# A chunk-of-four layout for the state-space scan, whole rest splits and earlier tables in a two-layer trunk

## The chip, the cores and the metric

The kernel runs on one core of a Trainium2 chip. The time is the device time of one execution in microseconds, the median of three runs. The core has five engines that run side by side: TensorE (PE, matmuls; its weight loads are listed apart as PEld), VectorE (DVE), ScalarE (ACT), GpSimd (POOL), and SyncE (SP), which here does nothing but issue transfers between DRAM and on-chip memory. Each engine works through its own queue in program order and waits on semaphores for the others.

## The reference

Two layers work on `x` of 256 positions by 2048 features. Each has one input projection whose columns feed two groups of heads, a GLU projection, an output projection and two RMSNorms. Cut to what matters here:

```
for l in range(DEPTH):                                   # 2 layers
    h = rmsnorm(x, pre_norm_g[l])
    q, k, v, z_att, u, z_ssm = split(h @ w_in[l])        # 2048 x 6144
    o_att = diff_attention(q, k, v, lam, rel_bias)       # 8 heads, two softmax maps each
    o_att = rmsnorm(o_att, subln_g[l]) * (1 - lam_init) * silu(z_att)
    y = s5_ssm(u, ...)                                   # 64 groups x 64 complex states
    g_val, g_gate = split(gelu(y) @ w_glu[l])
    o_ssm = g_val * sigmoid(g_gate) * silu(z_ssm)
    mix = concat(o_att, o_ssm) @ w_out[l]
    x = x + rmsnorm(mix, post_norm_g[l])

s5_ssm:  h[t] = a * h[t-1] + B u[t]   (a, h complex, t = 0..255),   y = Re(C h) + d * u
```

## The kernel before

**Precision and the half steps.** Weights and activations are float32, and the kernel multiplies them in three products of rounded parts: high part by high part, high by rest, rest by high. Weights stream once from DRAM in 512 KB pieces called half steps, 144 a layer (`s` = 0 to 143), 288 in all (`hs`). Per half step SP loads `raw`, six half steps ahead (`emit_dma(hs + 6)`, five buffers); ACT rounds it into `hi` (`emit_hi(hs + 2)`); DVE forms the rest `lo = raw - hi` (`emit_lo(hs + 2)`, lines 245 to 264); PE runs `main(hs)`: 24 matmuls of 256 columns for s below 48, 12 of 512 columns after. The order of a layer is u (s 0 to 15), q (16 to 31), k (32 to 47), v and za, zs, the GLU weights, the output weights. The activations are `hthi`/`htlo` in the first projection, `ghi`/`glo` for GLU, `mxhi`/`mxlo` for the output.

**What sets the order.** The instruction order of each engine is written out by the Python program. Side work (tables, attention, scan, normalisation) sits in generators: `hooks(l, s)` (lines 1081 to 1133) starts them at given half steps, `run_first` and `run_second` (lines 302 to 318) let each go on by a piece before and behind `main`. Work of DVE in many small operations (the scan, the tables `z_ops` and `g_ops`) is put in a list `weave`; `fill` (line 213) takes operations from it until a budget in estimated nanoseconds is spent. In the loop over `hs` (lines 1229 to 1232) the budget `bal` is what PE is expected to take less what DVE has been given already. When there is anything to weave, `lo` is formed in two operations of 512 columns with side work ahead, between and behind.

**The state-space part.** 256 positions are cut in 64 chunks of 4. The evacuation of `u` (line 919 on) writes the projected `u` by chunk; `u_store` (line 680) sends half of it to a DRAM tile `uds` (s = 11 and 17), and `u_load` (line 684) brings it back in eight transfers as `U`, laid out by channel group (s = 12 and 18). `prep_gen` builds tables from the layer's parameters: `wi` (from u to each chunk's contribution to the state) and `gc` (from state to y, `g_ops`, line 611, whose operations in layer 0 wait for `cmfree`). `s_gen` (line 718, started at s = 15) multiplies `U` by `wi` on PE into `pss`, in four groups of 64 matmuls, and ACT copies each into `H`: for every state 64 chunks. The last two groups wait for `u2` (s >= 20). `scan_ops` (line 753) then runs over the 64 chunks one after another, in 62 steps of four operations of 128 x 64, each reading chunk s-1 at a stride of 64 words. `y_gen` (line 766) turns `H` and `gc` into y, and ends in `ghi` and `glo`, one operation of 512 columns each. `pt` and `apow` hold powers of `a`, made once at the start for both layers in `pow_ops` (line 459).

Of the kernel before, what the change touches and what calls it, by code (L numbers as in the profile page):

```python
# [10 lines left out]
F32 = mybir.dt.float32  # L11
# [14 lines left out]
MAGIC = 12582912.0  # L26
SC = 70
Y0 = (80, 77)
# [3 lines left out]
PG = 1  # L32
CAP = 1500.0
RES = 0.0
SA = 51
# [4 lines left out]
PD = (1, 1)  # L40
F0 = 7
EB = 400
W3 = 4
# [15 lines left out]
def hybrid_trunk(ctx: ExitStack, tc, x, rel_bias, pre_norm_g, post_norm_g, w_in, lambda_q1, lambda_k1,  # L59
# [40 lines left out]
    def cost(o):  # L100
        n = 1
        for d in o.shape[1:]:
            n *= d
        load[0] += 68 + n / 0.96
        return 68 + n / 0.96

# [8 lines left out]
    def tt(o, a, b, op):  # L115
        V.tensor_tensor(o, a, b, op=op)  # L116
        return cost(o)
# [23 lines left out]
    apow = cp.tile([128, 2, 64, 4], F32, name="apow")  # L141
    a4s = cp.tile([128, 2, 64], F32, name="a4s")
    cf = cp.tile([128, 2, 64], F32, name="cf")
    nlam = cp.tile([128, 2], F32, name="nlam")
# [100 lines left out]
    def emit_lo(hs, budget, halves=False):  # L245
        if hs >= 2 * NCH:
            return
        src, hi = raw.pop(hs), split[hs][0]
        lo = late[hs] if hs in late else sp.tile([128, 1024], F32R, tag="lo", name="lo")
        hf = hi.bitcast(F32)  # L250
        if (weave and budget > 0) or urgent:
            budget = UB if urgent else budget
            fill(budget / 3)
            for p in range(2):
                c = slice(512 * p, 512 * p + 512)
                tt(lo[:, c], src[:, c], hf[:, c], ALU.subtract)
                fill(budget / 3)
        elif halves:
            for p in range(2):
                c = slice(512 * p, 512 * p + 512)  # L260
                tt(lo[:, c], src[:, c], hf[:, c], ALU.subtract)
        else:
            tt(lo, src, hf, ALU.subtract)
        split[hs] = (hi, lo)
# [133 lines left out]
    def params_ops(T, bt):  # L398
# [72 lines left out]
        S["pw"] = True  # L471

        lm = bt[0:2, 1536:1664].rearrange("p (a d) -> p a d", a=2)
        lv = bt[0:2, 512:768].rearrange("p (a b d) -> p a b d", a=2, b=2)
# [10 lines left out]
    def prep_gen(l, slots):  # L485
# [45 lines left out]
        weave.append(z_ops(l, bv, zt, tcn))  # L531
        if l:
            weave.append(g_ops(l, ccv, tcn, gslots))
        yield from until("z" + K)
# [16 lines left out]
        if l:  # L551
            yield from until("g" + K)
        else:
            weave.append(g_ops(l, ccv, tcn, gslots))
        wi = []
# [3 lines left out]
        for b0 in range(0, 8, nb):  # L559
# [11 lines left out]
            for b, ps in zip(range(b0, b0 + nb), pss):  # L571
                psv = ps.rearrange("p (h a g q) -> p h a g q", h=2, a=2, g=2)
                wv = wi[b // 4].rearrange("p (b h r a q) -> p b h r a q", b=4, h=2, r=2, a=2)[:, b % 4]
                for r in range(2):
                    for g in range(2):
                        act(wv[64 * g:64 * g + 64, :, r], psv[64 * r:64 * r + 64, :, :, g ^ r], AF.Copy)
            if l and b0 == WB - 1:
                for _ in range(WY):
                    yield
# [31 lines left out]
    def g_ops(l, ccv, tcn, gslots):  # L611
        while f"cmfree{l}" not in S:
            yield 100
        apl = [apow[:, a, 32 * l:32 * l + 32, :] for a in range(2)]
        gs = []
        for hf in range(2):
            gc = R(gslots[hf], "gc")
            gv = gc.rearrange("p (m a e c) -> p m a e c", m=16, a=2, e=4)
# [99 lines left out]
    def s_gen(l):  # L718
        yield from until(f"wi{l}")
        H = rp.tile([128, 2, NPAIR, 64], F32, tag="big", name="H")  # L720
# [3 lines left out]
        for b0 in range(0, 8, 2):  # L724
            while b0 >= 4 and not S["u2"]:
                yield
# [3 lines left out]
            for b in (b0, b0 + 1):  # L730
                wi = S[f"wi{l}"][b // 4]
                for h in range(2):
# [6 lines left out]
            for r, ps in enumerate(pss):  # L739
                psv = ps.rearrange("p (a j c) -> p a j c", a=2, j=4)  # L740
                act(H[:, :, 4 * b0 + r:4 * b0 + 8:2, 1:64], psv[:, :, :, 0:63], AF.Copy)
        yield
# [3 lines left out]
        for d in range(2):  # L746
# [3 lines left out]
            yield  # L750
        weave.append(scan_ops(l))

    def scan_ops(l):
        H = S["H"]
        ar = apow[:, 0, 32 * l:32 * l + 32, 3].unsqueeze(1).to_broadcast([128, 2, 32])
        ai = a4s[:, :, 32 * l:32 * l + 32]
        for s in range(2, 64):
            t1 = scp.tile([128, 2, 32], F32, tag="sc1", name="sc1")
            t2 = scp.tile([128, 2, 32], F32, tag="sc2", name="sc2")
            yield mul(t1, H[:, :, :, s - 1], ar) + SC  # L760
            yield mul(t2, H[:, ::-1, :, s - 1], ai)
            yield tt(t1, t1, H[:, :, :, s], ALU.add) + SC
            yield tt(H[:, :, :, s], t1, t2, ALU.add) + SC
        S[f"h{l}"] = True

    def y_gen(l, j):
# [43 lines left out]
        yield  # L810
        hv = S["ghi"].rearrange("p (b c i) -> p i b c", b=8, i=4)[:, :, 2 * j:2 * j + 2]
        lv = S["glo"].rearrange("p (b c i) -> p i b c", b=8, i=4)[:, :, 2 * j:2 * j + 2]
        yv = pg.rearrange("p (i b c) -> p i b c", i=4, b=2)
        act(hv, yv, AF.Copy)
        tt(lv, yv, hv.bitcast(F32), ALU.subtract)
        S[f"y{l}{j}"] = True
# [102 lines left out]
    def evac(l, seg, b, ac):  # L919
        if seg in ("U4", "u"):  # L920
            yield from until(f"rbc{l}")
            for j, a in enumerate(ac):
                bb = j if seg == "U4" else b
                o = S["u"].rearrange("p (m b c) -> p b c m", m=4, b=8)[:, bb]
                mul(o, a[:, 0:256].rearrange("p (c m) -> p c m", m=4),
                    rbc.rearrange("p (c m) -> p c m", m=4))
        elif seg in ("q", "k"):
# [153 lines left out]
    def hooks(l, s):  # L1081
# [20 lines left out]
        if s == 96 and l + 1 < DEPTH:  # L1102
            S["prep"] = prep_gen(l + 1, (8, (8, 2), (4, 3)))
            at(cur[0], S["prep"])
# [5 lines left out]
        if s == 11:  # L1110
            S["U"] = rp.tile([128, NPAIR, 64], F32, tag="U", name="U")
        if s in (11, 17):
            u_store(0 if s == 11 else 4)
        if s in (12, 18):
            u_load(0 if s == 12 else 4)
        if s == 15:
            at(cur[0], s_gen(l))
        if s == 21:
            at(cur[0], toep_gen(l))
        S["u2"] = s >= 20  # L1120
        S["zfree"] = s >= 113
# [18 lines left out]
    cur = [0]  # L1140
    BUDS = (2250.0, 2200.0)
    BUDL = 2140.0
    with tc.manual_schedule():
# [26 lines left out]
        at(PG, params_gen())  # L1170
        at(2, prep_gen(0, (3, (1, 7), (4, 8))))
        S["done"] = None
        bal = 0.0
        for hs in range(2 * NCH):
# [53 lines left out]
            run_first(hs)  # L1228
            bal = min(bal, CAP) + (BUDL if not l and s >= 44 else BUDS[l]) + pload[0] - load[0] - 1130
            load[0] = 0.0  # L1230
            emit_lo(hs + 2, 0 if s >= SX else min(bal, EB) if s < F0 else bal - RES)
            bal -= max(0.0, load[0] - 1130)
            held = hs in late or 2 * LAYER - LB <= hs < 2 * LAYER
# [57 lines left out]
```

## Time and profile before

| what | us |
|---|---|
| median of three runs | 926.35 (925.54 to 928.47) |
| profiled execution, of that its span | 926.7, 924.9 |
| PE busy, share of the span | 907.7, 98% |
| DVE busy, share of the span | 683.5, 74% |
| ACT busy, share of the span | 488.1, 53% |
| mean granted clock of TensorE | 0.994 |

The rows further down come from one profiled execution; its span runs from the first to the last instruction. "Busy" of an engine adds the time of its instructions and leaves out those that only issue transfers or signal. A row's idle time is what the engine spent waiting just ahead of it, with the engine and tile that ended the wait. The granted clock is given as a share of 2.4 GHz, so 0.5 is 1.2 GHz.

### The profile page before, as it was taken

What the parts mean: (1) busy time and instruction counts of PE and PEld (TensorE: products, weight loads), DVE (VectorE), ACT (ScalarE), POOL (GpSimd) and SP (SyncE); (2) the same over time, 40 slices, a digit from 0 to 9 for tenths busy, and PEclk for the clock granted to TensorE, in tenths of its full rate; (3) what the DMA queues carried; (4) which work ended last, traced back from release to release, by engine and by line L of the source; (5) the groups of instructions that cost most, each with busy time, mean ns of one, the idle gap of its engine ahead of it and who ended that gap; (6) DMA issues with size and microseconds to landing.
All of it is one profiled execution on the core that took longest, in us unless ns stands there. A gap on an engine that the chain in (4) does not pass through costs nothing.

```text
span 924.9 us, 17644 instructions
## 1 busy us (share of the span) xinstructions
PE 907.7 (98%) x6722; PEld 795.1 (86%) x6722; DVE 683.5 (74%) x1606; ACT 488.1 (53%) x881; POOL 17.2 (2%) x26
## 2 busy tenths in 40 slices
PE   9999999999999999999999999999999999999995
PEld 8999999888888788887889999997888788888884
DVE  4898686999995756877877449999966566665564
ACT  6643384455465667444468443335565655644451
POOL 3000000000000000000000000000000000000001
PEclk9999999999999999999999999999999999999998
DMA  9988656855654497576656866965556346665852
GB/s 303 209 231 244 185 165 172 278 158 168 184 155 137 126 232 243 171 249 201 215 173 193 230 175 168 246 187 165 163 156 183 115 137 203 197 210 168 291 183 91
DMA packets 187892, 177.21 MB, mean 192 GB/s; under 512 B 42550, under 2 KB 131184, under 8 KB 186912
## 3 DMA queue, kind: packets, MB, share of 16 engines
q1 hardware_dynamic: 187456, 175.96, 64.3%
q8 instruction: 53, 0.87, 0.4%
q14 instruction: 31, 0.25, 0.1%
q0 software_dynamic: 352, 0.13, 0.1%
HBM read 168.44 MB, written 7.88 MB: 191 GB/s over the span
## 4 chain that ended last, share of the span: by engine, by line
PE 87%; DVE 5%; ACT 3%; DMA 2%; SPq 1%; issue 1%; DVEq 0%; ACTq 0%
PE ac L113 79%; DVE lo L116 2%; DMA xt<-in_x_dram 1%; PE lga L113 1%; PE psy L113 1%; PE pss L113 1%; PE po L113 1%; SPq L496 1%; PE psw L97 1%; PE acu L113 1%; ACT junk L134 1%; DMA raw<-in_w_glu_dram 1%; ACT hi L134 1%; DMA raw<-in_w_in_dram 1%; ACT y L134 0%
## 5 line engine op out<-in xcount | busy, mean ns | idle before, releaser
L134 ACT ACTIVATE hi<-raw 128x1024 fp32r<-128x1024 f32 (+1 forms) x282 | 297.8, 1056 | 357.3 <-PE ac L113 272.2
L116 DVE TENSOR_TENSOR lo<-raw,hi 128x512 fp32r<-128x512 f32 (+1 forms) x401 | 359.8, 901 | 105.5 <-ACT hi L134 104.3
L113 PE MATMUL ac<-hthi,hi 128*128 128x256 f32 x736 | 211.7, 288 | 0.3 <-ACT hi L134 0.3
L113 PE MATMUL ac<-htlo,hi 128*128 128x256 f32 x736 | 209.4, 285 | 0.8 <-DVE htlo L123 0.5
L113 PE MATMUL ac<-hthi,lo 128*128 128x256 f32 x736 | 209.1, 284 | 0.6 <-DVE lo L116 0.5
L113 PE MATMUL ac<-hi,hthi 128*128 128x512 f32 x384 | 154.4, 402 | 0.0
L113 PE MATMUL ac<-lo,hthi 128*128 128x512 f32 x384 | 149.8, 390 | 0.4 <-DVE lo L116 0.4
L113 PE MATMUL ac<-hi,htlo 128*128 128x512 f32 x384 | 150.1, 391 | 0.0
L113 PEld LDWEIGHTS ac<-htlo,hi 128*128 128x128 f32 x736 | 141.8, 193 | 1.7 <-DVE htlo L123 1.7
L113 PEld LDWEIGHTS ac<-hthi,hi 128*128 128x128 f32 x736 | 141.7, 193 | 1.3 <-ACT hi L134 0.5
L113 PEld LDWEIGHTS ac<-hthi,lo 128*128 128x128 f32 x736 | 141.7, 193 | 1.2 <-DVE lo L116 1.2
L113 PE MATMUL ac<-lo,mxhi 128*128 128x512 f32 x228 | 89.0, 390 | 0.7 <-DVE lo L116 0.6
L113 PE MATMUL ac<-hi,mxhi 128*128 128x512 f32 x228 | 89.0, 391 | 0.0
L113 PE MATMUL ac<-hi,mxlo 128*128 128x512 f32 x228 | 88.7, 389 | 0.0
L113 PEld LDWEIGHTS ac<-hi,hthi 128*128 128x128 f32 x384 | 72.1, 188 | 16.1
L113 PEld LDWEIGHTS ac<-hi,htlo 128*128 128x128 f32 x384 | 72.1, 188 | 15.8
L113 PEld LDWEIGHTS ac<-lo,hthi 128*128 128x128 f32 x384 | 72.2, 188 | 14.6 <-DVE lo L116 0.8
L113 PEld LDWEIGHTS ac<-lo,mxhi 128*128 128x128 f32 x228 | 42.8, 188 | 10.3 <-DVE lo L116 1.5
L113 PE MATMUL ac<-hi,ghi 128*128 128x512 f32 x128 | 51.5, 403 | 0.0
L113 PEld LDWEIGHTS ac<-hi,mxlo 128*128 128x128 f32 x228 | 42.8, 188 | 8.9
L113 PE MATMUL ac<-lo,ghi 128*128 128x512 f32 x128 | 50.1, 391 | 0.3 <-DVE lo L116 0.3
L113 PEld LDWEIGHTS ac<-hi,mxhi 128*128 128x128 f32 x228 | 42.8, 188 | 8.9
(206 smaller groups left out, 1154.5 us busy)
## 6 DMA issues: line engine op xcount, KB each, us to landing
raw<-in_w_in_dram SPq DMA_DIRECT2D x191, 512.0 KB, 4.2
raw<-in_w_out_dram SPq DMA_DIRECT2D x64, 512.0 KB, 4.7
raw<-in_w_glu_dram SPq DMA_DIRECT2D x32, 512.0 KB, 4.3
U<-uds SPq DMA_DIRECT2D x48, 64.0 KB, 3.3
xt<-in_x_dram SPq DMA_DIRECT2D x8, 256.0 KB, 7.6
uds<-u SPq DMA_DIRECT2D x4, 512.0 KB, 6.0
pg<-in_post_norm_g_dram SPq DMA_DIRECT2D x2, 1024.0 KB, 7.1
xt<-in_x_dram SPq DMA_DIRECT2D x2, 1024.0 KB, 10.1
```

The source lines that it names most:

```text
L97: P.transpose(o, i, idn)
L113: P.matmul(o, lhsT=l, rhs=r, start=start, stop=stop, skip_group_check=True)
L116: V.tensor_tensor(o, a, b, op=op)
L134: A.activation(out=o, in_=i, func=f, **kw)
L496: SY.dma_start(out=bv[64 * d:64 * d + 64, a, r::2], in_=src[l].rearrange("(m r g) p c -> r g p m c", r=2, g=2)[r, d ^ r])
```

## The change

Five things change. The 64 chunks are laid out in `H` by their place in groups of four (position `i` in the four, then group `k`): the evacuation of `u` writes that order, and the copies to `H`, the writing of `ghi` and `glo` follow it. `scan_ops` then first joins the four chunks of each group for all 16 groups at once (12 operations of 128 x 1024 and a small copy), steps over the 16 groups (15 steps of four operations of 128 x 64, with `a16`, the 16th power, made by nine more operations in `pow_ops`), and finally carries the group states back into the chunks (12 operations of some 1024). `lo` is formed by one operation also while there is work to weave. The budget of DVE counts 147 ns and 1/0.955 ns a column for each operation, its cap is 1800, and separate settings for the first half steps go. `g_ops` follows `z_ops` directly, and only its second half waits for `cmfree`; `s_gen` waits for the first half of `wi` only (`wa`). The hooks move: `u_store` to s = 14 and 19, `u_load` to s = 15 and 20, `u2` to s >= 22.

On SP in layer 1, from the last loads of `raw` ahead of the first store of `u` to those behind the second load of `U`, the kernel before has:

```order
L206 DMA raw<-in_w_in_dram 128x8x128 x8
L682 DMA uds<-u 512x1x256
L206 DMA raw<-in_w_in_dram 128x8x128
L691 DMA U<-uds 16x4x256 x8
L206 DMA raw<-in_w_in_dram 128x8x128 x5
L682 DMA uds<-u 512x1x256
L206 DMA raw<-in_w_in_dram 128x8x128
L691 DMA U<-uds 16x4x256 x8
L206 DMA raw<-in_w_in_dram 128x8x128 x5
```

In the changed kernel the same place reads:

```order
L204 DMA raw<-in_w_in_dram 128x8x128 x11
L686 DMA uds<-u 512x1x256
L204 DMA raw<-in_w_in_dram 128x8x128
L695 DMA U<-uds 16x4x256 x8
L204 DMA raw<-in_w_in_dram 128x8x128 x4
L686 DMA uds<-u 512x1x256
L204 DMA raw<-in_w_in_dram 128x8x128
L695 DMA U<-uds 16x4x256 x8
L204 DMA raw<-in_w_in_dram 128x8x128 x3
```

Three more loads of `raw` stand ahead of the first store, and four in place of five between the first load of `U` and the second store.

On PE in the changed kernel, at the end of half step 159 (s = 15 of layer 1), where `pss` first reads `U` in that layer:

```order
L110 MATMUL ac<-hthi,hi 128x256
L110 MATMUL ac<-htlo,hi 128x256
L110 MATMUL ac<-hthi,lo 128x256
L110 MATMUL pss<-U,wi 64x64 x32
L110 MATMUL ac<-hthi,hi 128x256
L110 MATMUL ac<-htlo,hi 128x256
```

The group of `pss` has the same place as in the kernel before, behind the same half step; the second pair of groups stands two half steps later than before.

On DVE at the start of layer 0's scan (`sc` are its two temporaries, `k` the evacuation of a projection), the kernel before has:

```order
L116 TENSOR_TENSOR lo<-raw,hi 128x1024
L116 TENSOR_TENSOR sc_2293<-H,apow 128x64
L116 TENSOR_TENSOR sc_2294<-H,a4s 128x64
L116 TENSOR_TENSOR sc_2293<-sc_2293,H 128x64
L116 TENSOR_TENSOR H<-sc_2293,sc_2294 128x64
L116 TENSOR_TENSOR sc_2299<-H,apow 128x64
L116 TENSOR_TENSOR lo<-raw,hi 128x512
```

and the changed kernel (`sct` holds the joined groups):

```order
L113 TENSOR_TENSOR sct<-H,a4s 128x1024
L113 TENSOR_TENSOR sct<-H,apow 128x1024
L113 TENSOR_TENSOR lo<-raw,hi 128x1024
L113 TENSOR_TENSOR sct<-sct,H 128x1024
L113 TENSOR_TENSOR sct<-sct 128x1024
L120 SCALAR_TENSOR_TENSOR k<-ac,rbc 128x256
L113 TENSOR_TENSOR lo<-raw,hi 128x1024
```

About two wide operations of the scan now stand between one `lo` and the next, and `lo` is whole.

```diff
...
@@ -101,8 +98,8 @@
         n = 1
         for d in o.shape[1:]:
             n *= d
-        load[0] += 68 + n / 0.96
-        return 68 + n / 0.96
+        load[0] += 147 + n / 0.955
+        return 147 + n / 0.955
 
     def mm4(o, l, r, start, stop):
         n, m = r.shape[-1], l.shape[-1]
...
@@ -250,11 +248,9 @@
         hf = hi.bitcast(F32)
         if (weave and budget > 0) or urgent:
             budget = UB if urgent else budget
-            fill(budget / 3)
-            for p in range(2):
-                c = slice(512 * p, 512 * p + 512)
-                tt(lo[:, c], src[:, c], hf[:, c], ALU.subtract)
-                fill(budget / 3)
+            fill(budget / 2)
+            tt(lo, src, hf, ALU.subtract)
+            fill(budget / 2)
         elif halves:
             for p in range(2):
                 c = slice(512 * p, 512 * p + 512)
@@ -469,6 +465,15 @@
         V.tensor_copy(a4s[:, 1], pi[3])
         yield ts(a4s[:, 0], pi[3], -1.0, None, ALU.mult)
         S["pw"] = True
+
+        sr, si = pr[3], pi[3]
+        for dr, di in ((T("tt"), T("tn")), (a16[:, 0], a16[:, 2])):
+            yield mul(T("p2"), sr, sr)
+            yield mul(T("p3"), si, si)
+            yield tt(dr, T("p2"), T("p3"), ALU.subtract)
+            yield stt(di, sr, 2.0, si, ALU.mult, ALU.mult)
+            sr, si = dr, di
+        yield ts(a16[:, 1], a16[:, 2], -1.0, None, ALU.mult)
 
         lm = bt[0:2, 1536:1664].rearrange("p (a d) -> p a d", a=2)
         lv = bt[0:2, 512:768].rearrange("p (a b d) -> p a b d", a=2, b=2)
@@ -529,8 +534,7 @@
             zt = [R(5, "z0"), R(6, "z1")]
         tcn = R(cslot, "ztmp")
         weave.append(z_ops(l, bv, zt, tcn))
-        if l:
-            weave.append(g_ops(l, ccv, tcn, gslots))
+        weave.append(g_ops(l, ccv, tcn, gslots))
         yield from until("z" + K)
         yield 1
         ps = side("pst")
@@ -550,8 +554,6 @@
         S["cmfree" + K] = True
         if l:
             yield from until("g" + K)
-        else:
-            weave.append(g_ops(l, ccv, tcn, gslots))
         wi = []
         while l and not S["wfree"]:
             yield
...
@@ -609,11 +613,11 @@
         S[f"z{l}"] = True
 
     def g_ops(l, ccv, tcn, gslots):
-        while f"cmfree{l}" not in S:
-            yield 100
         apl = [apow[:, a, 32 * l:32 * l + 32, :] for a in range(2)]
         gs = []
         for hf in range(2):
+            while hf and f"cmfree{l}" not in S:
+                yield 100
             gc = R(gslots[hf], "gc")
             gv = gc.rearrange("p (m a e c) -> p m a e c", m=16, a=2, e=4)
             ms = slice(16 * hf, 16 * hf + 16)
@@ -716,19 +720,19 @@
         yield
 
     def s_gen(l):
-        yield from until(f"wi{l}")
+        yield from until(f"wa{l}")
         H = rp.tile([128, 2, NPAIR, 64], F32, tag="big", name="H")
         S["H"] = H
         G.memset(H[:, :, :, 0:1], 0.0)
         U = S["U"]
         for b0 in range(0, 8, 2):
-            while b0 >= 4 and not S["u2"]:
+            while b0 >= 4 and not (S["u2"] and f"wi{l}" in S):
                 yield
             yield 2
 
             pss = [side("pss") for _ in range(2)]
             for b in (b0, b0 + 1):
-                wi = S[f"wi{l}"][b // 4]
+                wi = S[f"wi{l}" if b >= 4 else f"wa{l}"][b // 4]
                 for h in range(2):
                     for a in range(2):
                         for r, g in ((0, 0), (1, 1), (1, 0), (0, 1)):
@@ -738,7 +742,10 @@
             yield
             for r, ps in enumerate(pss):
                 psv = ps.rearrange("p (a j c) -> p a j c", a=2, j=4)
-                act(H[:, :, 4 * b0 + r:4 * b0 + 8:2, 1:64], psv[:, :, :, 0:63], AF.Copy)
+                hv = H[:, :, 4 * b0 + r:4 * b0 + 8:2]
+                act(hv[:, :, :, 16:64], psv[:, :, :, 0:48], AF.Copy)
+                act(hv[:, :, :, 1:16], psv[:, :, :, 48:63], AF.Copy)
+        weave.append(scan_ops(l))
         yield
 
         src = uds.rearrange("(q g n) (m r) -> g m n q r", q=4, g=2, m=4)
@@ -748,19 +755,41 @@
                 r = 64 * d + 16 * m
                 SY.dma_start(out=dst[r:r + 16, 1::2], in_=src[1 - d, m, :, 1::2])
             yield
-        weave.append(scan_ops(l))
 
     def scan_ops(l):
+
+
         H = S["H"]
-        ar = apow[:, 0, 32 * l:32 * l + 32, 3].unsqueeze(1).to_broadcast([128, 2, 32])
-        ai = a4s[:, :, 32 * l:32 * l + 32]
-        for s in range(2, 64):
+        c = slice(32 * l, 32 * l + 32)
+        ar = apow[:, 0, c, 3].unsqueeze(1).unsqueeze(3).to_broadcast([128, 2, 32, 16])
+        ai = a4s[:, :, c].unsqueeze(3).to_broadcast([128, 2, 32, 16])
+        br = a16[:, 0, c].unsqueeze(1).to_broadcast([128, 2, 32])
+        bi = a16[:, 1:3, c]
+        sct = R((3, 8)[l], "sct")
+        T, u = (sct[:, 1024 * i:1024 * i + 1024].rearrange("p (a m k) -> p a m k", a=2, m=32) for i in range(2))
+        h = [H[:, :, :, 16 * i:16 * i + 16] for i in range(4)]
+        prev = h[0]
+        for i in range(1, 4):
+            yield mul(u, prev[:, ::-1], ai)
+            yield mul(T, prev, ar)
+            yield tt(u, u, h[i], ALU.add)
+            yield tt(T, T, u, ALU.add)
+            prev = T
+        V.tensor_copy(h[3][:, :, :, 0], T[:, :, :, 0])
+        yield 140
+        for k in range(1, 16):
             t1 = scp.tile([128, 2, 32], F32, tag="sc1", name="sc1")
             t2 = scp.tile([128, 2, 32], F32, tag="sc2", name="sc2")
-            yield mul(t1, H[:, :, :, s - 1], ar) + SC
-            yield mul(t2, H[:, ::-1, :, s - 1], ai)
-            yield tt(t1, t1, H[:, :, :, s], ALU.add) + SC
-            yield tt(H[:, :, :, s], t1, t2, ALU.add) + SC
+            yield mul(t1, h[3][:, :, :, k - 1], br) + SC
+            yield mul(t2, h[3][:, ::-1, :, k - 1], bi)
+            yield tt(t1, t1, T[:, :, :, k], ALU.add) + SC
+            yield tt(h[3][:, :, :, k], t1, t2, ALU.add) + SC
+        for i in range(3):
+            p, o, n = (h[i - 1], h[i], 16) if i else (h[3][:, :, :, 0:15], h[0][:, :, :, 1:16], 15)
+            yield mul(u[:, :, :, 0:n], p[:, ::-1], ai[:, :, :, 0:n])
+            yield mul(T[:, :, :, 0:n], p, ar[:, :, :, 0:n])
+            yield tt(o, o, u[:, :, :, 0:n], ALU.add)
+            yield tt(o, o, T[:, :, :, 0:n], ALU.add)
         S[f"h{l}"] = True
 
     def y_gen(l, j):
...
@@ -921,9 +951,9 @@
             yield from until(f"rbc{l}")
             for j, a in enumerate(ac):
                 bb = j if seg == "U4" else b
-                o = S["u"].rearrange("p (m b c) -> p b c m", m=4, b=8)[:, bb]
-                mul(o, a[:, 0:256].rearrange("p (c m) -> p c m", m=4),
-                    rbc.rearrange("p (c m) -> p c m", m=4))
+                o = S["u"].rearrange("p (m b e k) -> p b k e m", m=4, b=8, e=4)[:, bb]
+                cut = lambda t: t.rearrange("p (k e m) -> p k e m", e=4, m=4)
+                mul(o, cut(a[:, 0:256]), cut(rbc))
         elif seg in ("q", "k"):
             stt(S[seg][:, 256 * b:256 * b + 256], ac[0][:, 0:256], 0.125 if seg == "q" else 1.0, rbc, ALU.mult, ALU.mult)
         elif seg == "v":
...
@@ -1109,15 +1139,15 @@
                 SY.dma_start(out=S["xt"][t], in_=src[128 * t:128 * t + 128])
         if s == 11:
             S["U"] = rp.tile([128, NPAIR, 64], F32, tag="U", name="U")
-        if s in (11, 17):
-            u_store(0 if s == 11 else 4)
-        if s in (12, 18):
-            u_load(0 if s == 12 else 4)
+        if s in (14, 19):
+            u_store(0 if s == 14 else 4)
+        if s in (15, 20):
+            u_load(0 if s == 15 else 4)
         if s == 15:
             at(cur[0], s_gen(l))
         if s == 21:
             at(cur[0], toep_gen(l))
-        S["u2"] = s >= 20
+        S["u2"] = s >= 22
         S["zfree"] = s >= 113
         S["wfree"] = l > 0
         for h in range(8):
...
@@ -1226,10 +1256,10 @@
                 if s < 3:
                     residual(l - 1, 512 * s + 512, 256)
             run_first(hs)
-            bal = min(bal, CAP) + (BUDL if not l and s >= 44 else BUDS[l]) + pload[0] - load[0] - 1130
+            bal = min(bal, CAP) + (2880.0 if s < 48 else 2724.0) - SPARE[2 if l else int(s >= 44)] + pload[0] - load[0] - LOT
             load[0] = 0.0
-            emit_lo(hs + 2, 0 if s >= SX else min(bal, EB) if s < F0 else bal - RES)
-            bal -= max(0.0, load[0] - 1130)
+            emit_lo(hs + 2, 0 if s >= SX else bal)
+            bal -= max(0.0, load[0] - LOT)
             held = hs in late or 2 * LAYER - LB <= hs < 2 * LAYER
             main(hs, 0 if held else None)
             pload[0] = 0.0
```

## Rows read from the trace of the kernel before

**Rows 1.** The page: span, busy time of each engine, shares of the chain, one issue group.

```profile
span 924.9 us, 17644 instructions
PE 907.7 (98%) x6722; PEld 795.1 (86%) x6722; DVE 683.5 (74%) x1606; ACT 488.1 (53%) x881; POOL 17.2 (2%) x26
...
PE 87%; DVE 5%; ACT 3%; DMA 2%; SPq 1%; issue 1%; DVEq 0%; ACTq 0%
...
uds<-u SPq DMA_DIRECT2D x4, 512.0 KB, 6.0
```

**Rows 2.** Waits of PE's weight loads: what for, us in total, times, longest.

```profile
PEld ac L113 <- DVE lo L116: 4.2, 7, 1.0
...
PEld po L113 <- ACT wt L134: 2.0, 2, 1.4
PEld psx L97 <- DVE xt L123: 1.7, 1, 1.7
...
PEld ac L113 <- DVE htlo L123: 1.7, 4, 0.7
```

**Rows 3.** Windows: stretch, length, busy PE, PEld, DVE, ACT, POOL; clock, DMA share, GB/s.

```profile
157.00:270.00 113.00, 113.00 (x577) 93.44 (x576) 109.73 (x411) 59.68 (x121) 0.52 (x1) 1.00 0.63 192
...
560.00:660.00 100.00, 100.00 (x696) 92.15 (x695) 96.85 (x338) 44.38 (x68) 0.00 (x0) 1.00 0.68 189
```

**Rows 4.** Timeline of SP's queue, 507 to 541 us: start, duration, issue, count.

```profile
508.84 0.37 SPq L206 DMA_DIRECT2D raw<-in_w_in_dram  x1
509.27 0.58 SPq L682 DMA_DIRECT2D uds<-u  x1
...
514.52 4.05 SPq L691 DMA_DIRECT2D U<-uds  x8
...
526.54 0.59 SPq L682 DMA_DIRECT2D uds<-u  x1
...
533.25 4.11 SPq L691 DMA_DIRECT2D U<-uds  x8
```

**Rows 5.** The chain of waits, 514 to 532 us: start, duration, what.

```profile
513.90 9.96 PE ac L113 x83
523.86 1.09 PE pss L113 x64
```

**Rows 6.** Timeline of DVE, 514 to 525 us, the rest of half step 159.

```profile
516.23 1.23 DVE L116 TENSOR_TENSOR lo<-raw,hi 128x1024 fp32r<-128x1024 f32 x1 [1.65 <-ACT hi L134]
```

**Rows 7.** The tile U on SP, 514 to 519 us: its issues, their landing.

```profile
L691 SPq DMA_DIRECT2D U<-uds x8: 303/424/508, 514.5 to 518.3; - x8
...
DMA to landing us min/median/max: 2.1/3.2/4.0
```

**Rows 8.** Windows after two waits of PE, columns as in rows 3.

```profile
468.50:471.00 2.50, 2.35 (x12) 1.91 (x13) 1.75 (x5) 2.20 (x5) 0.00 (x0) 0.75 0.29 108
471.00:474.50 3.50, 3.50 (x24) 3.50 (x23) 2.20 (x4) 1.69 (x5) 0.00 (x0) 0.69 0.36 101
736.50:739.00 2.50, 1.50 (x11) 1.08 (x10) 2.38 (x5) 2.42 (x9) 0.00 (x0) 1.00 0.50 111
```

**Rows 9.** Groups of DVE: count, busy us, mean ns, idle us and releaser.

```profile
L116 DVE TENSOR_TENSOR lo<-raw,hi 128x1024 fp32r<-128x1024 f32 x161 | 196.0, 1222 | 90.8 <-ACT hi L134 90.3
L116 DVE TENSOR_TENSOR lo<-raw,hi 128x512 fp32r<-128x512 f32 x240 | 163.9, 686 | 14.6 <-ACT hi L134 14.0 <-issue 0.2
L116 DVE TENSOR_TENSOR sc<-H,apow 128x64 f32<-128x64 f32 x124 | 34.0, 274 | 2.8
...
L116 DVE TENSOR_TENSOR sc<-H,a4s 128x64 f32<-128x64 f32 x124 | 32.4, 261 | 0.0
...
L116 DVE TENSOR_TENSOR gc<-bt,apow 128x1024 f32<-128x1024 f32 x8 | 9.8, 1220 | 0.0
...
L116 DVE TENSOR_TENSOR u<-ac,rbc 128x256 f32<-128x256 f32 x14 | 7.8, 627 | 2.1 <-PE ac L113 2.1
...
L116 DVE TENSOR_TENSOR za<-za,po 128x256 f32<-128x256 f32 x16 | 6.7, 419 | 9.1 <-ACT junk L134 8.9
```

More of the change, by code (lines that the diff above doesn't have):

```diff
@@ L26 @@
 MAGIC = 12582912.0
-SC = 70
+SC = 57
 Y0 = (80, 77)
@@ L32 @@
 PG = 1
-CAP = 1500.0
-RES = 0.0
+CAP = 1800.0
 SA = 51
@@ L40 @@
 PD = (1, 1)
-F0 = 7
-EB = 400
 W3 = 4
@@ L142, in hybrid_trunk @@
     a4s = cp.tile([128, 2, 64], F32, name="a4s")
+    a16 = cp.tile([128, 3, 64], F32, name="a16")
     cf = cp.tile([128, 2, 64], F32, name="cf")
@@ L576, in prep_gen @@
                         act(wv[64 * g:64 * g + 64, :, r], psv[64 * r:64 * r + 64, :, :, g ^ r], AF.Copy)
+            if b0 + nb == 4:
+                S["wa" + K] = [w.rearrange("p (b i q) -> p b i q", b=4, i=8) for w in wi]
             if l and b0 == WB - 1:
@@ L810, in y_gen @@
         yield
[L811 to L815, printed above, removed]
+        hv, lv = (S[n].rearrange("p (b k e i) -> p b e i k", b=8, e=4, i=4) for n in ("ghi", "glo"))
+        yv = pg.rearrange("p (i b e k) -> p b e i k", i=4, b=2, e=4)
+        for b in range(2):
+            act(hv[:, 2 * j + b], yv[:, b], AF.Copy)
+        for b in range(2):
+            tt(lv[:, 2 * j + b], yv[:, b], hv.bitcast(F32)[:, 2 * j + b], ALU.subtract)
         S[f"y{l}{j}"] = True
@@ L1102, in hooks @@
         if s == 96 and l + 1 < DEPTH:
-            S["prep"] = prep_gen(l + 1, (8, (8, 2), (4, 3)))
+            S["prep"] = prep_gen(l + 1, (8, (8, 2), (3, 4)))
             at(cur[0], S["prep"])
@@ L1140, in hybrid_trunk @@
     cur = [0]
-    BUDS = (2250.0, 2200.0)
-    BUDL = 2140.0
+    SPARE = (150.0, 200.0, 300.0)
+    LOT = 1225.0
     with tc.manual_schedule():
@@ L1170, in hybrid_trunk @@
         at(PG, params_gen())
-        at(2, prep_gen(0, (3, (1, 7), (4, 8))))
+        at(2, prep_gen(0, (3, (1, 7), (8, 4))))
         S["done"] = None
```

## The prediction

> **What bounds the kernel now.** I read the page first. PE is busy 907.7 of 924.9 us, and 87% of the chain that ended last is PE [rows 1]. So the time falls only if PE waits less, and grows by whatever PE waits more. Then I read what PE's weight loads wait for (the loads run ahead of the matmuls, so these sums are upper ends of what the matmuls lose): 4.2 us for `lo` in 7 places, 2.0 for `wt`, 1.7 for `xt` at the layer boundary, 1.7 for `htlo` [rows 2]. Together that is 9.6 us in the whole run. Then I read stretches by window. From 157 to 270 us and from 560 to 660 us, where DVE scans, DVE is busy 109.73 of 113 and 96.85 of 100 us, and PE is busy all of it at full clock [rows 3]. A full DVE there costs nothing today. Last I read the queue of SP in layer 1, because the change moves two transfers there [rows 4].
>
> I number half steps 0 to 287; number 159 is s=15 of layer 1. PE takes 2.88 us for one of the projection (24 matmuls, about 0.12 each, as 83 of them fill 9.96 us [rows 5]).
>
> **The transfer of u, layer 1.** This is the large term. `u` goes to DRAM (`uds`) in one transfer and comes back as eight (`U`); the load waits on SP until the store has landed, and PE's first `pss` waits for all eight. Before: store issued at 509.27, first load at 514.52, eight loads issued in 4.05 us [rows 4]; `pss` follows the half step before it without a wait at 523.86 [rows 5]. After: the store is hooked at s=14 instead of 11 and the load at s=15 instead of 12, while `pss` keeps its place, right behind half step 159. So when can the store go now? SP issues in order, and ahead of the store stands the raw load of half step 164. With five raw buffers it waits until `lo` of 159 has read its buffer. That `lo` starts at 516.23 and takes 1.23 [rows 6]: 517.46. A raw issue takes some 0.4 us, as 508.84 to 509.27 shows [rows 4]: the store goes at 517.9.
>
> The store took 5.25 us in the first case (509.27 to the first load at 514.52) and 6.71 in the second (526.54 to 533.25) [rows 4]; the median of all four is 6.0 [rows 1]. The eight loads start within 3.8 us (514.5 to 518.3), and the last lands 2.1 to 4.0 us after its start [rows 7]: 5.9 to 7.8 us. So U is complete at 517.9 + 5.25 + 5.9 = 529.1 at the earliest and at 517.9 + 6.71 + 7.8 = 532.4 at the latest. PE stands ready at 523.86. The stall is 5.2 to 8.5 us, and PE can do nothing instead, since its queue is in order. I take the median store and the short loads, since an idle PE also asks for no new raw data: 517.9 + 6.0 + 5.9 - 523.86 = 5.9 us. Relief of DVE cannot bring the store forward: `lo` of 159 waited 1.65 us for ACT's `hi` [rows 6], not for DVE's other work. A lower stall needs a store that beats all of its rows; I put the low end at 4.
>
> The second pair: store from s=17 to 19, load from 18 to 20, `pss` from s=20 to 22. The first pair has 523.86 - 517.9 = 6.0 us from store to `pss`, with the `pss` behind the half step after the store's; the second has its `pss` two half steps later, 6.0 + 2 x 2.88 = 11.7 us, against 11.2 (5.25 + 5.9) to 14.5 (6.71 + 7.8) needed. Stall 0 to 2.8; with 6.0 + 5.9 it is 0.2, and I take 0.3. In layer 0 `pss` waits for the tables, which come long after both loads; the move is covered there and costs nothing.
>
> **What the stall does to the clock.** After PE waited at the layer boundary (1.7 us for `xt` [rows 2]) the granted clock reads 0.75 over 2.5 us and 0.69 over 3.5 us [rows 8]: part of that stretch ran at 1.2 GHz. Lost: 0.25 x 2.5 + 0.31 x 3.5 = 1.7 us. After the wait for `wt` inside 736.5 to 739 us, with PE busy 1.50 of 2.50, it stayed at 1.00 [rows 8]. A wait of 5.9 us is longer than both, so I take 1.7, with ends 0 and 3.4 (the same twice). The Trainium skill, "TensorE: Matmul & The Clock Gate", section "HAM oscillation — how this bites in real kernels", says that a matmul engine that idles in a DMA wait is put back to its cold clock and starts the next block slow. By that rule the term is not 0; by the row at 736.5 alone it would be, and the sum would be 1.7 lower.
>
> **The scan.** Before: 62 steps of four 64-wide operations per layer; per kind 124 at 274 down to 261 ns [rows 9], so 62 x 4 x 0.268 = 66.5 us a layer. After: 24 operations of about 1024, 15 x 4 of 64, a small copy. A 1024-wide operation on runs of 16 costs 1.22 us if it goes like `gc`, whose operands have runs of 16 too [rows 9]. 24 x 1.22 + 60 x 0.268 + 0.2 = 45.6 us a layer, 42 us less in both. The upper end: `u`, whose operand hops at every word, takes 627 ns for 256 words where `za` takes 419 [rows 9], half as much again; so 1.8 to 2.05 us an operation and a scan as long as before. Either way PE does not wait for DVE in these stretches [rows 3], so the gain is 0; full PE is the cover.
>
> **Weights' rest in one operation.** 240 halves of 686 ns become 120 of 1222 [rows 9]: 164.6 - 146.6 = 18 us of DVE. Here too only the waits for `lo` count, at most 4.2 us [rows 2]. DVE's budget is reckoned anew (exact cost, cap 1800), which lets more side work stand ahead of one `lo`; `lo` of 159 ends at 517.46 and its half step starts only about 523.86 - 2.88 = 521.0, so 3.5 us of lead cover it.
>
> **Tables without pause.** Layer 0's second half of `gc` is no longer issued in a burst at half step 130; part of the 4.2 us for `lo` goes, I take -1.0. Nine more 64-wide operations for a^16 at the start, up to 9 x 0.27 = 2.4 us [rows 9] beside the `htlo` waits: +0.1. The scan ends sooner, so layer 0's `y` work starts four half steps earlier and meets the softmax of the later heads; the exposed wait for `wt` (2.0 [rows 2]) has then a twin in layer 0: +0.5. `H` is written by 32 operations of ACT instead of 16; ACT is 53% busy [rows 1], I take 0.1. `ghi` and `glo` in halves: 0. The other waits for `lo` shift by 0.3 either way, and I take -0.2 since DVE has more room. Together -1.0 + 0.1 + 0.5 + 0.1 - 0.2 = -0.5; ends -6 (all of `lo`, and most of `htlo`, gone) and +3 (`wt` twice, `htlo` doubled).
>
> **Sum.** The profiled execution took 926.7: 924.9 of span and 1.8 around it; the median of the three runs is 0.35 lower. 926.7 + 5.9 + 0.3 + 1.7 - 0.5 = 934.1; on the median 933.7. This case's own range, with stall 4 to 8.5, clock 0 to 3.4 and small terms -3 to +1.5, not all at one end: 928.5 to 938.
>
> **Rivals.**
> 1. The stall is short and is paid by DVE relief: no change. The store would have to land in 3 us and the loads in 4, with the clock kept: a stall of 517.9 + 7.0 - 523.86 = 1.0, and 926.35 + 1.0 - 0.5 = 926.9. Against it: the rows of the store, 5.25 and 6.71 [rows 4]. For it: with PE standing, the raw buffers fill and their loads pause. By the Trainium skill, "DMA: Bandwidth & Descriptors", section "Anatomy of one DMA — SWDGE (gpsimd) path", a transfer takes 2.0 us plus its bytes at 436 GB/s, an estimate of 3.2 us for these 512 KB; the stall would be 5.9 - 2.8 = 3.1 and the time 930.9. That fit is for another path of issue; the trace says 5.25 at least, and I follow it.
> 2. The other side, faster: relief of DVE ends the waits for `lo` and `htlo`, and U is there when PE comes. It decides only if U lands before 524; then 926.35 - 4.2 x 0.6 - 1.0 = 922.8. For it: 60 us less DVE work. Against it: no PE wait lies in the scan stretches [rows 3], and a landing before 524 asks for a store and eight loads within 6 us of 517.9, where the issues alone take 4.05 [rows 4].
> 3. The wide scan operations run at the rate of hopping words and are reckoned too cheap, 1.22 instead of 2.05: 48 operations each push a `lo` back by up to 0.83 us. If every sixth shows, 48 x 0.83 / 6 = 6.6 us on top of the forecast: 940. Against it: `gc`'s 1.22.
>
> **Chances.** A change below 0.3%, some 2.8 us, can't be told from none. The forecast 0.82, rival 1 0.07, rival 2 0.04, rival 3 0.07. The forecast's own low end and rival 1 share the middle: faster 0.05, same 0.09, slower 0.86. Range 928.0 to 938.0; below it lie rivals 1 and 2, above it rival 3.
>
> **What would show it.** Right: in layer 1 a `pss` of 5 to 7 us wait on the DMA of `U` just behind s=15, a store issued about 6 us ahead of it, and a granted clock under 1.00 for a few us behind it; DVE some 60 us less busy and PE no sooner through 157 to 270; `sct` operations at 1.22 us. Wrong: no wait at `pss`; or a wait of several us at the second `pss` of layer 1 or at layer 0's; or PE busy much less than all of 560 to 660; or `sct` at 2 us.

## The result, and the profile after

| | median us | range, runs |
|---|---|---|
| before | 926.9 | 925.54 to 928.47, 4 |
| changed | 934.92 | 934.42 to 936.1, 4 |

The ratio is 1.0088, 95% interval 1.0068 to 1.0107: slower by 8 us, against a forecast of 933.7 (928 to 938). The page of the changed kernel, in the lines that answer to [rows 1]:

```profile
span 933.1 us, 17158 instructions
PE 907.9 (97%) x6722; PEld 796.0 (85%) x6722; DVE 660.2 (71%) x1178; ACT 489.0 (52%) x905; POOL 17.2 (2%) x26
...
PE 89%; DMA 3%; ACT 3%; DVE 2%; SPq 2%; issue 1%; DVEq 0%; ACTq 0%
...
uds<-u SPq DMA_DIRECT2D x4, 512.0 KB, 5.6
```

PE does the same work, 907.9 us against 907.7, in a span 8.2 us longer; DVE does 23 us less; and the chain that ends last has DMA at 3% where it had 2%. So PE waits more, and for transfers. What PE's matmuls of the changed kernel wait for (us in total, times, longest; `psx` takes `x` into the next layer at the layer boundary, `po` is an attention product that reads the softmax weights `wt`):

```profile
PE pss L110 <- DMA U<-uds: 5.5, 2, 4.2
PE ac L110 <- DVE htlo L120: 2.2, 2, 1.8
PE psx L94 <- DVE xt L120: 1.5, 1, 1.5
PE po L110 <- ACT wt L131: 1.4, 2, 1.0
...
PE pss L110 <- ACT H L131: 1.0, 2, 0.7
PE ac L110 <- DVE lo L113: 0.6, 2, 0.4
```

The first line is new and the largest. Its place is shown by the chain of waits of the changed kernel from 512 to 545 us (start, duration, what), where [rows 5] had nothing but PE:

```profile
515.42 1.07 ACT hi L131
...
516.51 1.24 DVE lo L113
...
517.76 0.37 SPq L204
...
518.17 6.19 DMA uds<-u
...
524.43 0.33 SPq L695
...
527.62 2.32 DMA U<-uds
...
530.07 1.98 PE pss L110 x62
532.05 4.18 PE ac L110 x24
```

Read it from the top: `hi`, then `lo` of half step 159, then the raw load that waited for it, then the store of `u`, then eight loads one behind the other, then `pss`. Two of its matmuls started at 528.4 on the first loads; the other 62 had to wait until 530.07. The 24 matmuls of the next half step take 4.18 us; in the same place before they took 3.07. Why, the windows of the changed kernel show (length, busy PE, PEld, DVE, ACT, POOL, granted clock, DMA share, GB/s):

```profile
526.00:530.00 4.00, 0.45 (x2) 0.29 (x2) 0.37 (x1) 0.00 (x0) 0.00 (x0) 0.72 0.52 143
530.00:534.00 4.00, 3.93 (x71) 3.84 (x72) 0.00 (x0) 1.20 (x4) 0.00 (x0) 0.50 0.85 236
534.00:538.00 4.00, 4.00 (x87) 3.80 (x86) 0.76 (x1) 1.67 (x4) 0.00 (x0) 0.93 0.00 0
```

For the 4 us behind the wait PE ran at 1.2 GHz. Lost: 0.50 x 3.93 + 0.07 x 4.0 = 2.2 us.

Where the 8.2 us arise, by the start of the first matmul of a half step (changed minus before, us, worked out from both traces): half step 8: +1.3; 42: +2.8; 95: +2.8; 132: +1.8; 145: +0.4; 159: +0.3; 168: +8.2; 287: +8.2. Between 159 and 168 lies nearly all of it; what came and went ahead of that is taken up below.

DVE where it scans, to [rows 3], and the groups of DVE that answer to [rows 9] (count, busy us, mean ns, idle):

```profile
157.00:270.00 113.00, 113.00 (x586) 93.94 (x585) 96.23 (x221) 59.30 (x118) 0.52 (x1) 1.00 0.66 199
560.00:660.00 100.00, 100.00 (x753) 93.72 (x744) 86.94 (x164) 43.08 (x64) 0.00 (x0) 1.00 0.71 190
```

```profile
L113 DVE TENSOR_TENSOR lo<-raw,hi 128x1024 fp32r<-128x1024 f32 x280 | 341.2, 1221 | 127.0 <-ACT hi L131 125.7
...
L113 DVE TENSOR_TENSOR sct<-H,a4s 128x1024 f32<-128x1024 f32 x6 | 7.3, 1221 | 5.6 <-ACT H L131 5.6
```

The wide operations run at 1.22 us, DVE is 13.5 and 9.9 us less busy in these stretches, and PE is as full as before.

### The profile page after: what moved, and what is told of

Same layout as the page of the kernel before. It is cut to its first block, busy times and chain, and to the rows that moved or that the text cites. A ratio compares the mean times of both kernels' runs of the same rounds, so it can differ in the third digit from the quotient of the medians.

```text
span 933.1 us, 17158 instructions
## 1 busy us (share of the span) xinstructions
PE 907.9 (97%) x6722; PEld 796.0 (85%) x6722; DVE 660.2 (71%) x1178; ACT 489.0 (52%) x905; POOL 17.2 (2%) x26
## 4 chain that ended last, share of the span: by engine, by line
PE 89%; DMA 3%; ACT 3%; DVE 2%; SPq 2%; issue 1%; DVEq 0%; ACTq 0%
PE ac L110 80%; DMA raw<-in_w_in_dram 1%; PE lga L110 1%; PE acu L110 1%; PE po L110 1%; PE psy L110 1%; PE pss L110 1%; SPq L501 1%; PE psw L94 1%; ACT hi L131 1%; DMA raw<-in_w_glu_dram 1%; DMA uds<-u 1%; DVE lo L113 1%; ACT y L131 0%; PE pwt L94 0%
## 5 line engine op out<-in xcount | busy, mean ns | idle before, releaser
L113 DVE TENSOR_TENSOR lo<-raw,hi 128x1024 fp32r<-128x1024 f32 (+1 forms) x282 | 342.6, 1217 | 127.8 <-ACT hi L131 126.5
```

## The experiments

The theory is the forecast's: the late transfer of `u` makes PE wait at the first `pss` of layer 1. The rival: the rest of the change (scan, whole rests, tables, earlier y) makes the waits. All ratios are to the kernel before, run on the same chip, with 95% intervals.

**Hooks put back in the changed kernel.**

```diff
-        if s in (14, 19):
-            u_store(0 if s == 14 else 4)
-        if s in (15, 20):
-            u_load(0 if s == 15 else 4)
+        if s in (11, 17):
+            u_store(0 if s == 11 else 4)
+        if s in (12, 18):
+            u_load(0 if s == 12 else 4)
-        S["u2"] = s >= 22
+        S["u2"] = s >= 20
```

> The changed kernel with only the hooks of the transfer of u put back (store at s=11 and 17, load at s=12 and 18, second groups of pss from s=20). Theory H, the late transfer costs it all: the changed kernel's 934.9 us less the stall at pss (5.9) and the slow stretch behind it (1.3 to 1.7) and some 0.5 at the second pair: 926 to 928 us, no PE wait for U, level with the kernel before. Rival S, the scan, whole rests and tables cost it: 933 to 935 us with the waits spread over DVE and ACT.

928.46 us against 928.22, ratio 1.0013 (1.0001 to 1.0024). Its chain around the first `pss` of layer 1:

```profile
513.97 11.28 PE ac L110 x94
525.24 1.09 PE pss L110 x64
```

No wait is left there, and 7 of the 8 us are gone, by the ratios. The other parts of the change gain nothing in sum; by this ratio they lose about 1 us, and its interval only just leaves out a loss of nothing.

**Only the hooks moved, in the kernel before.** The reverse of that edit.

> The kernel before with only the hooks of the transfer of u moved as in the change (14, 19, 15, 20, 22). Theory H: 926.9 + 5.9 + 1.3 to 1.7 = 934 to 935 us, with the wait at the first pss of layer 1. Rival S: 927 to 928 us, the wait is then made by something else of the change.

934.5 us against 928.22, ratio 1.0077 (1.0059 to 1.0096), with one new line among the waits of its matmuls:

```profile
PE pss L113 <- DMA U<-uds: 4.7, 2, 3.5
```

The hooks alone make nearly all of the loss, 0.77% of 0.88%. The rival falls, as the cause of the 8 us.

**The wait, or the transfers.** The transfers stay late, and `pss` of layer 1 starts later.

```diff
-        if s == 15:
+        if s == (18 if l else 15):
             at(cur[0], s_gen(l))
```

> The changed kernel, transfers left late, but in layer 1 the matmuls into pss start at s=18 instead of 15, three half steps (8.6 us) later. Theory H, it is the position of the wait in PE's queue: U lands about 530, pss is reached about 532.6, so no wait and 926.5 to 928.5 us. Rival D, the transfers themselves disturb the stream of weights (eight loads and a store in the way of raw): the time stays above 932 us.

927.97 us, ratio 0.9999 (0.9985 to 1.0012). U is complete at 529.9 us as before, and PE is not there yet:

```profile
524.91 8.52 PE ac L110 x71
533.43 1.09 PE pss L110 x64
```

The late transfer costs nothing that shows by itself. What costs is an instruction that needs it, early in a queue that runs in order.

**The distance.** The first store and load one half step earlier (s = 13 and 14), one profiled run.

```diff
-        if s in (14, 19):
-            u_store(0 if s == 14 else 4)
-        if s in (15, 20):
-            u_load(0 if s == 15 else 4)
+        if s in (13, 19):
+            u_store(0 if s == 13 else 4)
+        if s in (14, 20):
+            u_load(0 if s == 14 else 4)
```

> The changed kernel with the first pair of the transfer one half step earlier (store at s=13, load at s=14). If the wait is the distance from store to pss: it shrinks by one half step, 5.9 - 2.9 = 3.1 us, and U lands as long after the store as before (11.8 us). If the store or loads are what is slow there (a queue that frees late): the wait stays above 5 us.

931.0 us. Its chain there:

```profile
516.74 5.08 DMA uds<-u
...
525.10 2.40 DMA U<-uds
527.63 1.16 PE pss L110 x62
```

From half step 159 to 161 PE takes 10.32 us, against 16.15 in the changed kernel and 8.22 in the kernel before. So 2.1 us are lost, not 3.1: the store landed in 5.08 us, not 6.19. PE waited for `U` for 1.7 us, against 5.5, and the clock stayed at 1.00 behind this shorter wait:

```profile
531.00:535.00 4.00, 4.00 (x89) 3.80 (x88) 1.23 (x1) 2.26 (x5) 0.00 (x0) 1.00 0.39 101
```

Of the 5.8 us between this kernel and the changed one the half step of distance makes 2.9, the faster store 1.1 and the clock some 2. That the store was faster is what one run showed; why stays open.

**The clock by itself.** Idle matmuls on constants take the place of the wait.

```diff
+            if l and not b0:
+                w = side("warm")
+                for _ in range(24):
+                    mm(w[:, 0:128], ones, ones, True, True)
             pss = [side("pss") for _ in range(2)]
```

> The changed kernel with 24 idle matmuls of 128 columns on constants (some 5.1 us) just ahead of the first pss of layer 1, so that PE works while it would have waited. If the low clock behind the wait is due to the idle time and costs 1.3 to 1.7 us: granted clock 1.00 behind the wait and 933.2 to 933.8 us. If the clock falls there anyway, or the low clock costs nothing because something else bounds that stretch: 934.5 to 935.5 us. If the matmuls run longer than the wait: above 935.5.

933.5 us against 928.22, ratio 1.007 (1.005 to 1.0091). The windows behind the place where PE waited:

```profile
526.00:530.00 4.00, 4.00 (x47) 3.88 (x50) 0.76 (x1) 0.00 (x0) 0.00 (x0) 1.00 0.60 161
530.00:534.00 4.00, 4.00 (x92) 3.80 (x87) 0.00 (x0) 1.24 (x5) 0.00 (x0) 1.00 0.71 195
```

The clock stays at 1.00. From the start of half step 159 to that of 169 PE takes 40.0 us, against 42.3 in the changed kernel: 2.3 less, some 0.6 of them because `pss` began that much sooner after half step 159. So the slow clock comes from the idle time, and costs 1.7 to 2.2 us beside it. The medians agree with that (1.0070 against 1.0088), but their intervals overlap.

**The scan.** The changed kernel with the hooks back, and the 62 steps of the kernel before over the new layout:

```diff
-        for i in range(1, 4):
-            yield mul(u, prev[:, ::-1], ai)
...
+        at_ = lambda s: 16 * (s % 4) + s // 4
+        for s in range(2, 64):
+            p, q = at_(s - 1), at_(s)
+            yield mul(t1, H[:, :, :, p], ar) + SC
+            yield mul(t2, H[:, ::-1, :, p], ai)
+            yield tt(t1, t1, H[:, :, :, q], ALU.add) + SC
+            yield tt(H[:, :, :, q], t1, t2, ALU.add) + SC
```

> The changed kernel with the hooks of u put back and the scan as before, 62 steps of four 64-wide operations, over the new layout of the chunks. Forecast's step: the scan in fours saves some 42 us of DVE and nothing of the time, since PE does not wait in those stretches: level with the kernel with the hooks back alone (928.5, within 1.5 us). Rival: the longer DVE work delays rests and tables and PE waits for them: 931 us or more.

929.25 us, ratio 1.0006 (0.9994 to 1.0018), level with the scan in fours. The page:

```profile
PE 906.5 (98%) x6722; PEld 795.1 (86%) x6722; DVE 683.7 (74%) x1504; ACT 489.0 (53%) x905; POOL 17.2 (2%) x26
```

DVE does 23.3 us more than with the hooks back alone (660.4), and the time does not move. That DVE's busy time fell by less than the 42 us that I worked out has a plain reason: the record of one operation of DVE overlaps that of the next, so for many short ones count times mean is more than the time they fill. Added up record by record, DVE has 725.1 us with the hooks back and 766.6 with the old scan (worked out from both traces), 41.5 apart, as forecast; the time that is filled is 23.3 apart.

**Rests in halves.**

```diff
-            fill(budget / 2)
-            tt(lo, src, hf, ALU.subtract)
-            fill(budget / 2)
+            fill(budget / 3)
+            for p in range(2):
+                c = slice(512 * p, 512 * p + 512)
+                tt(lo[:, c], src[:, c], hf[:, c], ALU.subtract)
+                fill(budget / 3)
```

> The changed kernel with the hooks of u put back and the rests in two operations of 512 again where there is side work. Forecast's step: the 18 us of DVE that the single operation saves are off the path, so this is level with the kernel with the hooks back alone (within 1 us). Rival: the single operation removes waits of PE for lo, then this is 2 to 4 us slower.

932.4 us, ratio 1.005 (1.0034 to 1.0066): slower by 3 to 4 us than with whole rests, as the rival had it. The waits of its matmuls:

```profile
PE pss L110 <- issue: 3.2, 1, 3.2
PE ac L110 <- DVE lo L113: 2.6, 5, 1.3
```

Only part is the rival's mechanism: waits for `lo` grew to 2.6 us. The larger line is a stop of 3.2 us within a `pss` group of layer 0 that no semaphore explains. It ends at 144.8 us, and the granted clock over 144 to 148 us is 0.59. A transfer of 1536 KB (`tabs`, from which the attention bias is made) was in flight from 134.5 to 145.3; but in the kernel with the hooks back it was in flight too, from 137.8 us for 11.0, without such a stop, so it isn't enough to cause one. The profiled execution was also the slowest of the nine (935.5 us), so it isn't known whether the stop is in the others. The edit also leaves the budget at the cost of one operation (1225 ns) though two cost more, so it is not the rest by itself. What the whole rest is worth alone stays open; that it is worth nothing, as I forecast, is not borne out.

**The waits that remain.** Five versions go after the two new waits: `htlo` at 29.4 us and `H` near 133 us. The first bounds the side work of DVE in the first half steps by 400 ns:

```diff
-            emit_lo(hs + 2, 0 if s >= SX else bal)
+            emit_lo(hs + 2, 0 if s >= SX else min(bal, 400.0) if s < 7 else bal)
```

> The changed kernel with the hooks of u put back and, in the first seven half steps of a layer, at most 400 ns of side work around one rest, as in the kernel before. Theory: the 2.1 us wait for htlo at 29.7 us, and the 1.5 us of low clock that followed it in the run with the hooks back, come from the table work now put ahead of htlo there: 2 to 3.6 us under the kernel with the hooks back alone, a ratio of 0.997 to 0.999 to the kernel before. Rival: the table work then comes later and makes a wait of the same size at the next htlo or at the tables: no gain.

930.26 us, ratio 1.003 (1.001 to 1.005): a miss, no gain (the interval overlaps that of the hooks put back alone). The wait for `htlo` went (0.3 us left), and others took its place:

```profile
PE ac L110 <- DVE lo L113: 1.7, 4, 0.8
...
PE pss L110 <- issue: 1.2, 1, 1.2
...
PE acu L110 <- DVE lo L113: 0.8, 1, 0.8
PE ac L110 <- DVE u L113: 0.7, 1, 0.7
```

(`acu` is an accumulator like `ac`.) Two things took the place. The table work had to be done anyway; put off, it stood ahead of `u` at 45 us. The waits near 41 us have another cause, the weights themselves:

```profile
39.89 1.06 ACT L131 ACTIVATE hi<-raw 128x1024 fp32r<-128x1024 f32 x1 [6.99 <-DMA raw<-in_w_in_dram]
40.98 1.23 DVE L113 TENSOR_TENSOR lo<-raw,hi 128x1024 fp32r<-128x1024 f32 x1 [4.75 <-ACT hi L131]
```

ACT and DVE stood idle there until `raw` landed, at 39.8 us. PE came to half step 8 3.6 us sooner than with the hooks back alone (36.7 against 40.3), and was 0.9 us ahead at half step 14. Next, with it, one more half step between the groups of `pss` in layer 0 (added behind the copies into `H`):

```diff
+            if not l:
+                yield
```

> The same, and in layer 0 one more half step between two groups of pss, so that ACT's copies into H (two a bank instead of one) are done when PE asks for the bank. Theory: the two waits of pss for H (0.9 and 0.4 us near 134 us) go, 1 to 1.5 us under the kernel without it. Rival: ACT is behind with other work there and PE waits at the next step; or the later scan is late for y: no gain or a loss.

927.92 us, ratio 1.0002 (0.9989 to 1.0016). The waits for `H` are gone, and the stop of 1.2 us within `pss` too, in the one execution that was profiled. Then the same with 1000 ns in place of 400, and that with `Y0 = (84, 77)`:

> The changed kernel with the hooks back, one more half step between groups of pss in layer 0, and at most 1000 ns (not 400, not without bound) of side work around one rest in the first seven half steps of a layer. Theory: the two waits of pss for H (1.3 us) go, and half of the wait for htlo at 29.7 us (1 us, with the low clock behind it) without the later waits that 400 ns brought near 41 and 46 us: 925 to 927 us. Rival: what is taken from the head comes back where the tables are due: 928 us or more.

> The same with the y work of layer 0 started four half steps later (s=84), where it stood in the kernel before. Theory: the wait for wt near 285 us (0.6 us) and the waits for lo at 315 to 318 us (0.5 us) come from the earlier y work: 0.5 to 1 us under the kernel without it. Rival: y is then late for ghi and the GLU half steps wait: 1 us over it or more.

927.06 us, 0.9993 (0.9981 to 1.0004), and 926.85 us, 0.999 (0.9979 to 1.0002). The first is at the upper end of its range; against the hooks put back alone its ratio is 0.2% lower. The second's step is in the right direction and inside the noise. Last, the additional half step only behind the first group (`if not l and not b0`), where PE had waited:

> The version with the hooks back, the bound of 1000 ns at the head and y at s=84, but with the additional half step only between the first and the second group of pss in layer 0, where PE waited for H, so that the scan starts two half steps sooner. Theory: the waits of PE for lo between 244 and 251 us (1.8 us), where the later scan meets the softmax work, go, and the wait for H stays away: 925 to 926.5 us, 0.998 to the kernel before. Rival: the third or fourth group then waits for H instead, or the lo waits stay: 926.5 to 928 us.

925.41 us against 927.87, ratio 0.9974 (0.9963 to 0.9985). The waits of its matmuls, all of them (`warm` are matmuls on constants at the start):

```profile
PE psx L94 <- DVE xt L120: 1.5, 1, 1.5
PE ac L110 <- DVE lo L113: 1.2, 2, 0.8
PE warm L110 <- DVE sso L1179: 1.1, 1, 1.1
PE po L110 <- ACT wt L131: 1.0, 1, 1.0
PE ac L110 <- DVE u L113: 0.7, 1, 0.7
PE ac L110 <- DVE htlo L120: 0.5, 1, 0.5
PE psx L94 <- DMA xt<-in_x_dram: 0.2, 1, 0.2
```

This version has the scan, the whole rests and the tables of the change, and beats both kernels: 2.4 us under the kernel before. Which part makes the 2.4 us is not shown: neither the scan nor the whole rests nor the tables were taken out of this version, and the bound of 1000 ns was not tried in the kernel before, which has 400.

## Why the prediction held, and where it did not

- **The stall.** Forecast: store at 517.9, landing 6.0 later, loads 5.9 more, `pss` at 529.8, a stall of 5.9. Measured: 518.17, 6.19, 5.7, 530.07, and 5.5 us of waiting. The chain has every link that was named, and the hooks alone reproduce it.
- **The clock.** Forecast 1.7 from the layer boundary; measured 2.2 by the windows, 1.7 by the kernel that kept PE busy. The forecast took it from another place of the program and the size held. It had read that other fall somewhat high: half step 144 took 5.18 us there, against 3.74 in the changed kernel at full clock, which is 1.4.
- **The second pair.** Forecast 0.3, measured none: `pss` does not wait there.
- **The scan.** 1.22 us an operation and nothing in the time; rival 3 is out. DVE was given 13.5 and 9.9 us of room in the two stretches and PE had no wait there to lose, as [rows 3] said. One sign was read wrongly: DVE is 23 us less busy, not some 60, since the forecast added up overlapping records.
- **The small terms** were the weak step: -0.5 in the forecast, +0.3 at half step 159, and made up quite differently. Ahead of `htlo` I had taken +0.1; it came to 2.2 us of waiting against 0.5 before (`PE ac L113 <- DVE htlo L123: 0.5, 1, 0.5`). I had priced the nine operations for a^16, and not that the new budget lets some table work of the first half steps go ahead of `htlo`. The copies into `H` were to cost 0.1 and cost 1.0, since I looked at ACT's share of the whole run and not at the one stretch where `pss` follows at once. The burst at half step 130 went, as forecast (-1.0; PE is 0.9 us better off from half step 131 to 132), and the wait for `wt` got its twin in layer 0 (0.5 us at 284.7 us, forecast +0.5). The rest of the balance is luck: in the profile of before the clock fell at the layer boundary [rows 8], in that of the changed kernel it did not (1.00 from 468 to 476 us), which is 1.4 us.
- **Rival 2** (DVE relief is the gain) fell for this change. With the hooks back and the two new waits taken away a version of it is 2.4 us under the kernel before, so there is a gain that the new waits hid; that it is relief of DVE, and not the edits that came with that version, is not shown.

## What to carry to other kernels

When a transfer is moved, work out the distance from its issue to the first instruction that needs it, link by link, with the landing times of the trace, and look at where that instruction stands in its queue; a gain elsewhere does not shorten it. Relief of an engine that nobody waits for is worth nothing at that place, but a new rule for handing out its time moves waits elsewhere, above all at the head of the program. Price an added operation by the stretch that it falls in, not by its engine's share of the run.

## What the runs showed of the hardware

The same idle time at the same place of the program lowers the clock in some executions and not in others. The 1.5 us wait at the layer boundary was followed by a slow half step (5.2 us in place of 3.7) in 3 of 14 profiles, and the wait of 1.7 to 1.8 us for `htlo` near 29.5 us, which 7 of the kernels have, by one (6.9 in place of 5.4) in 4 of 7. Here are two windows of the kernel with the hooks back, and behind them the same stretch of the changed kernel, whose instructions there are the same. In the 3 us ahead of them PE was busy for 1.16 us in both:

```profile
30.00:33.00 3.00, 3.00 (x19) 3.00 (x19) 2.73 (x11) 0.46 (x1) 0.00 (x0) 0.64 1.13 231
33.00:36.00 3.00, 3.00 (x23) 3.00 (x22) 2.55 (x13) 1.26 (x3) 0.00 (x0) 0.79 1.18 237
```

```profile
30.00:33.00 3.00, 3.00 (x27) 3.00 (x27) 2.73 (x12) 0.24 (x2) 0.00 (x0) 1.00 1.22 238
33.00:36.00 3.00, 3.00 (x27) 3.00 (x26) 3.00 (x16) 1.63 (x3) 0.00 (x0) 1.00 1.20 247
```

Each such fall is worth 1.5 us, so two profiles can differ by that over a stretch in which their instructions are the same, and a wait of 1.5 to 1.8 us is dearer on average than it looks. Behind the waits of 5.5 and 4.7 us for U the clock fell in both profiles that have them; behind the 1.7 us there it did not, in the one that has it.
